# Products with V one unit later in the last third of the neighbourhood attention, and the weight groups' sums of squares moved into a score's bank

## The chip, the core and the metric

The kernel runs on one NeuronCore of a Trainium2 chip. The core has TensorE (PE, matrix products into PSUM), VectorE (DVE), ScalarE (ACT), GpSimd (POOL) and SyncE (SP, which here only issues DMAs). Each engine takes its instructions in the order in which the program gives them. The metric is the device time of one execution in microseconds (us); three executions of the kernel before gave 583.09, 578.28 and 580.79 us, median 580.79 us.

## The reference

One encoder layer over 1024 tokens of width 1024, cut to what matters here:

```python
def reference(x, norm_gain, w_in, q_norm_a, k_norm_a, na_rpb, w_out, final_norm_gain):
    h = _rmsnorm(x, norm_gain[l])
    proj = h @ w_in[l]
    q_a, k_a, v_a, g_a, q_b, k_b, v_b, g_b = jnp.split(proj, split_at, axis=-1)
    ...
    o_a = _gqa_blocked(q_a, k_a, v_a) * jax.nn.silu(g_a)
    o_b = _neighbourhood_attn(q_b, k_b, v_b, na_rpb[l])   # scores + bias, masked softmax, times V
    o_b = o_b * jax.nn.silu(g_b)
    mixed = jnp.concatenate([o_a, o_b], axis=-1)
    x = x + mixed @ w_out[l]
    return _rmsnorm(x, final_norm_gain)
```

Group A is full attention with 8 query heads over 2 key heads, group B attention over a window of the token grid with 8 heads of 64.

## The kernel before, in words

Every float32 operand of a product is split into two 16-bit parts, and a product is made of three 16-bit products (high·high, high·low, low·high). Weights come in 17 groups of 256 columns (0 to 12 from w_in, 13 to 16 from w_out), 1 MB each, loaded by POOL (L206) into two buffers. For each group ACT squares the raw weights in four quarters (`squares`, L349); PE adds the squares over the partitions with four one-column matmuls (`prep_b`, L364, "the sum"); DVE reads the result (L366) and POOL makes a scale of it (L367). Then ACT and DVE make the group's two parts (`split`, L390 and L395), and when these are done the next raw load may start.

After the projections and group A's attention comes group B's, in 64 *units*: one head of one block of 128 queries, the blocks in the order 0, 7, 1, 2, 3, 4, 5, 6 (`ORDER`), against 256 keys in the first 16 units and 384 in the rest. The program goes through *slots*; slot i does for unit i the softmax's first half (`b_qk`), for unit i-1 the rest (`b_lo`), and for unit i-5 the product with V (`b_pv`; 5 is `SKEW_B`). Step by step, for one unit:

- PE: scores, in every second slot for two units at once (`b_scores`, L801 and L804), each in one of four PSUM banks "sb";
- DVE: bias and maximum (L818), scale (L820); ACT: two exponentials (L821, L822); DVE: the low part (L827), into one of five buffers `t`;
- SP: a DMA transpose of both parts (L829) into one of five buffers `ptb`;
- PE: 6 or 9 matmuls with V (L842 to L844), four units in one of two PSUM banks "pvb"; after the fourth, DVE divides by the sums (L852 to L855) and POOL multiplies by the gate (L857). If the gate's part is not there yet, this evacuation is put off by a slot, and while it is, `late["held"]` keeps sums back.

When both halves of a block's mixed row are there, `os_start` squares, scales and splits the row (L880 to L898) and SP transposes it (L905). The output projection then multiplies it by the groups 13 to 16 (L480, tiles `po`), DVE adds the product to the residual (L953) and so frees the PSUM tile, of which there are two; ACT squares the row (L974), POOL takes the root (L982), DVE scales it (L985) and SP stores it (L986).

The order on PE is written by hand: in each slot the scores, then 2.4 *chunks* of six matmuls of pending projections ("fill"), then the product with V. A sum comes after the end of a tile or of a slot, if nothing is held, in the pvb bank that is not in use at the moment, in column 264+g (`spare[-1]`). ACT's and DVE's side work is handed out by a planner (`Flow`) that gives each slot a budget; what is due or urgent goes first. After the last unit a scheduler orders DVE, ACT, POOL and SP, and the fill that is left goes on: first the rows of block 4, then of 5 (`ORDER[5]`, `ORDER[6]`: blocks 4 and 5), at last of block 6, whose own row ends the kernel.

Of the kernel before, what the change touches and what calls it, by code (L numbers as in the profile page):

```python
# [16 lines left out]
P = 128  # L17
KC = 8
NU = 8
GC = 256  # L20
# [9 lines left out]
FILL_B = []  # L30
FILL_B_END = 2.4
SPLIT_AT = (8, 16, 24, 32, 40, 48, 56)
X2_BEHIND = {0: (0, 1), 1: (2,), 2: (3,), 3: (4,), 4: (5,), 5: (6,), 6: (7,)}
# [104 lines left out]
def kernel(ctx: ExitStack, tc: tile.TileContext, x: bass.AP, w: bass.AP, wo: bass.AP,  # L138
# [203 lines left out]
    def squares(g, delay):  # L342

        wss[g] = [tn(f"wss{g}_{k}", 1, "ws") for k in range(4)]

        def quarter(i):
            o = (carve(ar, 16384 + SLOTS["th"][0] + (turn.get("th", 0) + 1) % 2 * SLOTS["th"][1], [512], BF16)
                 if "b" in late else va_more)
            act.activation(o.rearrange("p (k c) -> p k c", c=GC), raw[g][:, QUARTERS[i]], AF.Square, accum_out=wss[g][i])  # L349
            if i == 3:  # L350
                job("act", 0, pend.append, g, delay=1, late=0, key=("sq", g))
        for i in range(4):
            job("act", 0.75 if g < 13 else 1.0, quarter, i, delay=delay, late=3 if g < 13 else 1.2, key=("sq", g))
# [4 lines left out]

    def prep_b(g):
        pt = spare[-1][:, 264 + g:265 + g]  # L360
        top = [a.bitcast(BF16)[:, 1:2] for a in (mh[:, :1], *wss[g])]
        n = len(wss[g])
        for i in range(n):
            pe.matmul(pt, top[0].to_broadcast([P, P]), top[1 + i], start=i == 0, stop=i == n - 1)  # L364
        t = wss[g][0]
        dve.tensor_scalar(t, pt, -2.0 ** -27, 1e-30, op0=OP.mult, op1=OP.add)  # L366
        pool.tensor_tensor(col(S_ + g), t, mh[:, :1], op=OP.pow)  # L367
        scaled.add(g)
# [82 lines left out]
    def sums_now(force=False):  # L451

        while pend and (force or late.get("head", 2) == 2 and (pend[0] < 3 or fl.slot >= late.get("again", 0)) and not late.get("held")):
            g = pend.pop(0)
# [339 lines left out]
    def b_scores(u, hs):  # L794
# [4 lines left out]
        for h in hs:  # L799
            sbs[u, h] = bank("sb")[:, :n * P]  # L800
            pe.matmul(sbs[u, h], q[h], khh[:, h, ks], start=True, stop=False)  # L801
        for h in hs:
            r = slice(h % 2 * D, h % 2 * D + D)
            pe.matmul(sbs[u, h], q[h][r], late["klo"][r, h // 2, ks], start=False, stop=True)  # L804

    def b_qk(i, u, h):
# [18 lines left out]
    def b_lo(i, u, h):  # L825
        hl, t = hls.pop(("b", u, h))
        dve.tensor_tensor(hl[:, 1], t, hl[:, 0], op=OP.subtract)  # L827
        pt = slot("ptb", [P, 2 * keys(u)[1], P], F16)
        sp.dma_start_transpose(pt, hl.rearrange("p a b -> p (a b)"))  # L829
        pts["b", u, h] = pt  # L830

    def b_pv(i, u, h):
# [12 lines left out]
        if h % 4 == 3:  # L845
            def evac():
                late["held"] = (u // 2, hh * GC) not in ready
                if late["held"]:
                    job("dve", 0.85, evac, late=0)
                    return  # L850
# [229 lines left out]

    def run_units(units, skew, qk, lo, pvf, n, hooks=None, by_hand=0):

        m, hand = len(units), ExitStack()
        for i in range(m + skew):
            if i == by_hand:
                hand.enter_context(tc.manual_schedule(engines={e.engine for e in (act, dve, pool, sp)}))
            first = (lambda: qk(i, *units[i])) if i < m else None
            second = (lambda: lo(i - 1, *units[i - 1])) if 1 <= i <= m else None
            last = (lambda: pvf(i - skew, *units[i - skew])) if i >= skew else None
            if qk is a_qk:  # L1090
# [65 lines left out]
    def hooks2(i):  # L1156
        hooks(i)
        for u, k in zip(ORDER, SPLIT_AT):
            if i - SKEW_B == k:
                at(1, "post", os_start, u)  # L1160
# [3 lines left out]
    fl.base = BASE_B  # L1164
    with run_units(ub, SKEW_B, b_qk, b_lo, b_pv, rates(FILL_B, FILL_B_END), hooks2):
        pass
# [92 lines left out]
```

## Time and profile before

| | |
|---|---|
| profiled execution, whole | 580.6 us |
| its span in the trace | 578.8 us |
| PE busy | 520.2 us, 90% |
| DVE busy | 458.5 us, 79% |
| ACT busy | 391.7 us, 68% |
| granted TensorE clock, mean | 0.972 of 2.4 GHz |
| group B's units, first scores to last | 370.4 to 520.8 us |

The engines' busy shares are averages over stages; group B's stage is read by itself below. In a timeline row the first number is the start in us from the span's start, the second the duration, the bracket the idle time of the engine before the row and what ended it.

### The profile page before, as it was taken

Reading aid. Unit: us, or ns where it says so; the run is one execution under the profiler, and the core shown is the slowest. Engines: PE = TensorE matmul, PEld = TensorE weight load, DVE = VectorE, ACT = ScalarE, POOL = GpSimd, SP = SyncE. Lnnn points to the kernel's source line nnn. Section 1 sums busy time; section 2 is a strip of 40 time slices with the busy share of each in tenths; the row PEclk is TensorE's granted clock in tenths of the full one; section 3 lists DMA queues with packets and bytes.
Section 4 is the critical chain, followed back from the end, with each engine's and each line's share of the span. In section 5 each row is a group of like instructions: output and inputs, shape, how many; then the busy total and the mean of one; then the engine's idle time right before and its main releaser. Section 6 shows DMA issues by size and latency. Waiting matters only on the chain. (4 is left out here: it accounts for less than half of the span.)

```text
span 578.8 us, 13970 instructions
## 1 busy us (share of the span) xinstructions
PE 520.2 (90%) x5583; PEld 404.1 (70%) x5583; DVE 458.5 (79%) x1018; ACT 391.7 (68%) x615; POOL 150.1 (26%) x181
## 2 busy tenths in 40 slices
PE   2678989969999999999999999997989988897894
PEld 0456867757887555568888888885867766786783
DVE  4688687989887987878789888577988998888742
ACT  5555456668777759686786867395889987775210
POOL 2395786650000000000000024333412220111300
PEclk9978999998999999999999999997989999999898
DMA  9989548779999999998999989234397999979732
GB/s 241 224 163 233 119 114 155 129 146 166 210 218 193 156 216 185 199 190 160 235 169 198 195 177 179 96 74 111 64 180 158 210 170 171 158 148 189 156 73 73
DMA packets 245539, 95.49 MB, mean 165 GB/s; under 512 B 236513, under 2 KB 237025, under 8 KB 243554
## 3 DMA queue, kind: packets, MB, share of 16 engines
q1 hardware_dynamic: 241874, 73.89, 71.5%
q0 software_dynamic: 3312, 19.92, 12.6%
q8 instruction: 43, 0.70, 0.5%
q10 hardware_dynamic: 288, 0.79, 0.5%
q14 instruction: 22, 0.18, 0.1%
HBM read 29.56 MB, written 4.19 MB: 58 GB/s over the span
## 5 line engine op out<-in xcount | busy, mean ns | idle before, releaser
L480 PE MATMUL pj<-whl,hT 128*128 128x256 f16 x2112 | 258.4, 280 | 22.1 <-DMA hT<-ar 7.5
L480 PEld LDWEIGHTS <-hT 128*128 128x128 f16 x2112 | 205.7, 100 | 61.6 <-issue 18.2
L720 ACT ACTIVATE ar<-s,nm,sm 128x1024 f32<-128x1024 f32 x64 | 76.9, 1201 | 55.6 <-DVE nm L718 55.3
L718 DVE CUSTOM_DVE_ANT_0 ar<-s,sm 128x1024 bf16<-128x1024 f32 x64 | 82.0, 1281 | 34.2 <-PE s L713 33.8
L480 PEld LDWEIGHTS <-ar 128*128 128x128 f16 x768 | 73.1, 99 | 16.1 <-issue 6.8
L726 DVE TENSOR_TENSOR ar<-ar 128x1024 f16<-128x1024 f32 x64 | 80.3, 1254 | 0.9 <-ACT ar L721 0.8
L480 PE MATMUL po<-whl,ar 128*128 128x256 f16 x576 | 70.0, 277 | 3.1 <-DVE x L953 2.3
L721 ACT ACTIVATE ar<-ar 128x1024 f16<-128x1024 f32 x64 | 67.6, 1057 | 1.9
L821 ACT ACTIVATE rq<-ar,mx,sm 128x384 f32<-128x384 f32 (+1 forms) x64 | 43.0, 672 | 25.0 <-DVE mx L820 25.0
L822 ACT ACTIVATE ar<-ar,mx,sm 128x384 f16<-128x384 f32 (+1 forms) x64 | 43.5, 680 | 2.1
L480 PE MATMUL kb<-hT,whl 128*128 128x512 f16 x192 | 44.5, 379 | 0.0
L711 PE MATMUL s<-kTa,rq 128*128 128x512 f16 x128 | 38.5, 383 | 2.6 <-ACT ar L720 2.4
L827 DVE TENSOR_TENSOR ar<-rq,ar 128x384 f16<-128x384 f32 (+1 forms) x64 | 35.7, 557 | 6.1 <-ACT ar L822 6.0
L744 PE MATMUL pv<-va,ar 128*128 128x64 f16 x384 | 40.3, 194 | 0.0
L743 PE MATMUL pv<-va,ar 128*128 128x65 f16 x384 | 40.2, 193 | 0.0
L745 PE MATMUL pv<-va,ar 128*128 128x65 f16 x384 | 40.0, 192 | 0.0
L743 PEld LDWEIGHTS <-ar 128*128 128x128 f16 x384 | 35.7, 97 | 5.5 <-issue 0.3
L744 PEld LDWEIGHTS <-ar 128*128 128x128 f16 x384 | 35.5, 97 | 5.5 <-issue 0.3
L395 DVE SCALAR_TENSOR_TENSOR whl<-raw,sm,whl 128x512 f16<-128x512 f32 x52 | 38.4, 771 | 0.2 <-ACT whl L390 0.2
L206 POOL DMA_DIRECT2D raw<-in_w_dram x11 | 6.7, 607 | 112.8 <-ACT ar L721 88.7
L745 PEld LDWEIGHTS <-ar 128*128 128x128 f16 x384 | 35.6, 99 | 0.0
L390 ACT ACTIVATE whl<-raw,sm 128x512 f16<-128x512 f32 x52 | 33.8, 708 | 0.0
(163 smaller groups left out, 916.1 us busy)
## 6 DMA issues: line engine op xcount, KB each, us to landing
raw<-in_w_dram POOLq DMA_DIRECT2D x11, 1024.0 KB, 7.7
raw<-in_wo_dram POOLq DMA_DIRECT2D x4, 1024.0 KB, 5.8
ar<-in_x_dram SPq DMA_DIRECT2D x7, 512.0 KB, 6.2
khh<-ar SPq DMA_DIRECT2D x16, 128.0 KB, 3.5
x2b<-in_x_dram POOLq DMA_DIRECT2D x4, 512.0 KB, 6.2
x<-in_x_dram POOLq DMA_DIRECT2D x4, 512.0 KB, 6.9
out_dram<-x2b SPq DMA_DIRECT2D x8, 256.0 KB, 3.5
ar<-ar SPq DMA_TRANSPOSE x112, 4.4
```

Of the source, the lines that this page charges most:

```text
L395: dve.scalar_tensor_tensor(wp[g][1][:, q], raw[g][:, q], col(S_ + g), wp[g][0][:, q], op0=OP.mult, op1=OP.subtract)
L480: pe.matmul(*o[0], **o[1])
L711: pe.matmul(s[:, c * 512:(c + 1) * 512], q, kTa[:, 4 * c:4 * c + 4, hh], start=True, stop=False)
L718: dve.tensor_tensor_reduce(out=hl[:, 1].bitcast(BF16), in0=s, in1=col(SHA).to_broadcast([P, 1024]), scale=col(NSA), scalar=3e38, op0=OP.ad ...
L720: act.activation(p32, s, AF.Exp, bias=nm, scale=col(SCA))
L721: at(0, "mid", lambda: act.activation(hl[:, 0], p32, AF.Copy))
L726: dve.tensor_tensor(hl[:, 1], p32, hl[:, 0], op=OP.subtract)
L743: pe.matmul(o, pt[:, kt], va[:, kt, hh, v_hi], start=kt == 0, stop=False)
L744: pe.matmul(o[:, :D], pt[:, kt], va[:, kt, hh, v_lo], start=False, stop=False)
L745: pe.matmul(o, pt[:, 8 + kt], va[:, kt, hh, v_hi], start=False, stop=kt == 7)
L821: act.activation(p32, t, AF.Exp, bias=mx, scale=col(SCB + hh))
L822: act.activation(hl[:, 0], t, AF.Exp, bias=mx, scale=col(SCB + hh))
```

## The change

Two things, and what they need.

1. From slot 40 on (`MORE`) the product with V of unit i-6 stands in slot i in place of i-5; slot 40 has none, and there is one slot more at the end. For the sixth transposed unit a buffer is added: every sixth unit from 40 on goes to the place of the second gate buffer "th", and from slot 38 on the squares' waste output keeps to the first.
2. In group B a sum is issued right behind a pair's scores, in the bank of the second of them (column 400+g), and no more at the end of tiles and slots. `late["held"]` goes; a group's sum may come two slots after its last square in place of one.

```diff
+MORE = 40
@@ squares
-            o = (carve(ar, 16384 + SLOTS["th"][0] + (turn.get("th", 0) + 1) % 2 * SLOTS["th"][1], [512], BF16)
+            o = (carve(ar, 16384 + SLOTS["th"][0] + (0 if "six" in late else (turn.get("th", 0) + 1) % 2) * SLOTS["th"][1], [512], BF16)
...
-                job("act", 0, pend.append, g, delay=1, late=0, key=("sq", g))
+                job("act", 0, pend.append, g, delay=2 if "b" in late else 1, late=0, key=("sq", g))
@@ prep_b
-    def prep_b(g):
-        pt = spare[-1][:, 264 + g:265 + g]
+    def prep_b(g, pt=None):
+        if pt is None:
+            pt = spare[-1][:, 264 + g:265 + g]
@@ sums_now
-        while pend and (force or late.get("head", 2) == 2 and (pend[0] < 3 or fl.slot >= late.get("again", 0)) and not late.get("held")):
+        while pend and (force or "b" not in late and late.get("head", 2) == 2 and (pend[0] < 3 or fl.slot >= late.get("again", 0))):
@@ b_scores
-            sbs[u, h] = bank("sb")[:, :n * P]
+            at_s = bank("sb")
+            sbs[u, h] = at_s[:, :n * P]
...
+        if pend:
+            g = pend.pop(0)
+            prep_b(g, at_s[:, 400 + g:401 + g])
+            try_split(g)
@@ b_lo
-        pt = slot("ptb", [P, 2 * keys(u)[1], P], F16)
+        k = i - MORE + 5
+        pt = (area(32896, [2 * keys(u)[1], P], F16) if k >= 0 and k % 6 == 5 else
+              slot("ptb", [P, 2 * keys(u)[1], P], F16))
@@ b_pv
-                late["held"] = (u // 2, hh * GC) not in ready
-                if late["held"]:
+                if (u // 2, hh * GC) not in ready:
@@ run_units
-        for i in range(m + skew):
+        for i in range(m + skew + (more < 1000)):
+            back = skew + (i >= more)
...
-            last = (lambda: pvf(i - skew, *units[i - skew])) if i >= skew else None
+            last = (lambda: pvf(i - back, *units[i - back])) if i >= back and i != more else None
@@ hooks2
+        if i == MORE - 2:
+            late["six"] = True
         for u, k in zip(ORDER, SPLIT_AT):
-            if i - SKEW_B == k:
+            if i - SKEW_B - (i >= MORE) == k:
                 at(1, "post", os_start, u)
```

The built order, at the three places of which the prediction speaks. First PE, where group 13's sum stands (`wss`: the squares' partial sums, `pvb` and `sb`: banks of the products with V and of the scores). Before, behind the product with V of slot 11, ahead of the scores of units 12 and 13:

```order
L844 MATMUL pvb_5110<-ar 128x65
L364 LDWEIGHTS mh
L364 MATMUL pvb_5109<-wss_0_5041,mh 128x1
L364 LDWEIGHTS mh
L364 MATMUL pvb_5109<-wss_1_5042,mh 128x1
...
L801 LDWEIGHTS qTb_109
L801 MATMUL sb_5107<-khh,qTb_109 128x256
```

Now, behind the scores of units 8 and 9:

```order
L807 LDWEIGHTS qTb_107
L807 MATMUL sb_5107<-klo,qTb_107 128x256
L366 LDWEIGHTS mh
L366 MATMUL sb_5107<-wss_0_5041,mh 128x1
L366 LDWEIGHTS mh
L366 MATMUL sb_5107<-wss_1_5042,mh 128x1
...
L482 LDWEIGHTS hT_99
L482 MATMUL pj_0_5293<-whl_4862,hT_99 128x256
```

It has moved up by almost four slots and out of the pvb bank. The others: group 12 from slot 7 to slot 0, group 14 from slot 23 to 18, group 15 from slot 27 to 24; group 16 from just ahead of slot 40's scores to just behind them. The four raw loads of w_out follow: on POOL the third stands now ahead of the first block's row scale (L887, L895 now), some four units earlier.

Second ACT, the squares of group 14 (`wss_0` to `wss_3`; `mx_h` names the unit by its head). Before:

```order
L349 ACTIVATE ar,wss_1_5419<-raw_5416 128x512
L821 ACTIVATE rq<-ar,mx_0_5642,sm 128x384
...
L349 ACTIVATE ar,wss_2_5420<-raw_5416 128x512
L821 ACTIVATE rq<-ar,mx_2_5720,sm 128x384
L822 ACTIVATE ar<-ar,mx_2_5720,sm 128x384
L349 ACTIVATE ar,wss_3_5421<-raw_5416 128x512
L821 ACTIVATE rq<-ar,mx_3_5746,sm 128x384
```

Now:

```order
L350 ACTIVATE ar,wss_2_5394<-raw_5390 128x512
L828 ACTIVATE rq<-ar,mx_6_5575,sm 128x256
L829 ACTIVATE ar<-ar,mx_6_5575,sm 128x256
L888 ACTIVATE mhl_5586,os_5585<-ar 128x512
L350 ACTIVATE ar,wss_3_5395<-raw_5390 128x512
L828 ACTIVATE rq<-ar,mx_7_5619,sm 128x256
```

The last square has moved from ahead of unit 19 to ahead of unit 15. Group 15's last square likewise stands now ahead of unit 21.

Third DVE at the end of the units (L852, now L860: evacuation of a pvb bank, `sumb_1` of the last four units; L953, now L961: residual, `po_15` of block 3). Before:

```order
L852 RECIPROCAL sumb_1_7657<-pvb_5110 128x4
L853 TENSOR_TENSOR sumb_1_7657<-sumb_1_7657,sm 128x4
L855 TENSOR_TENSOR ar<-pvb_5110,sumb_1_7657 128x256
L985 SCALAR_TENSOR_TENSOR x2b<-x2b,of_7002,gain_o 128x512 x2
L962 TENSOR_TENSOR rw_13_7586<-os_7130,sm 128x1
L953 SCALAR_TENSOR_TENSOR x_6421<-po_15_7483,rw_15_7484,x_6421 128x256 x2
```

Now:

```order
L961 SCALAR_TENSOR_TENSOR x_6421<-po_15_7470,rw_15_7471,x_6421 128x256 x2
...
L961 SCALAR_TENSOR_TENSOR x_6421<-po_13_7569,rw_13_7570,x_6421 128x256
L989 TENSOR_SCALAR of_6993<-of_6993 128x1
L860 RECIPROCAL sumb_1_7687<-pvb_5110 128x4
L993 SCALAR_TENSOR_TENSOR x2b<-x2b,of_6993,gain_o 128x512 x2
...
L961 SCALAR_TENSOR_TENSOR x_6421<-po_13_7569,rw_13_7570,x_6421 128x256
L989 TENSOR_SCALAR of_7495<-of_7495 128x1
L863 TENSOR_TENSOR ar<-pvb_5110,sumb_1_7687 128x256
```

The residual of block 3 stands now ahead of the last evacuation, not behind it, and the evacuation's last step stands behind one L993 pair more. On PE the product of unit 63 with V has 18 more fill matmuls ahead of it (12 and 6, of the rows of block 4), and 234 in place of 252 output matmuls behind it.

## Rows read from the trace of the kernel before

**Rows 1.** The waits of PE over the whole span: line, what was waited for, total us, times, longest.

```profile
PE pvb L842 <- DMA ar<-ar: 11.2, 7, 2.8
...
PE pvb L364 <- DVE ar L855: 3.0, 1, 3.0
```

**Rows 2.** Timeline of PE from slot 11's end to unit 16's scores.

```profile
397.14 0.25 PE L364 MATMUL pvb<-wss,mh 128*128 128x1 bf16 x4 [2.99 <-DVE ar L855]
397.25 0.59 PE L801 MATMUL sb<-khh,qTb 128*128 128x256 f16 x2
...
398.10 4.02 PE L480 MATMUL pj<-whl,hT 128*128 128x256 f16 x18
...
404.16 0.38 PE L801 MATMUL sb<-khh,qTb 128*128 128x256 f16 x2
...
408.34 0.49 PE L801 MATMUL sb<-khh,qTb 128*128 128x384 f16 x2
```

**Rows 3.** Busy time by stretch: PE, PEld, DVE, ACT, POOL (with instruction counts), granted clock, DMA share, GB/s. Columns: stretch, its length, then these.

```profile
397.00:404.10 7.10, 6.96 (x49) 4.86 (x49) 3.57 (x14) 3.42 (x7) 3.44 (x4) 0.57 0.30 55
...
542.60:549.60 7.00, 6.96 (x49) 5.59 (x49) 5.41 (x23) 2.77 (x6) 1.08 (x2) 0.76 0.56 161
```

**Rows 4.** Timeline of DVE ahead of the evacuation that PE waited for.

```profile
388.93 2.74 DVE L395 SCALAR_TENSOR_TENSOR whl<-raw,sm,whl 128x512 f16<-128x512 f32 x4 [0.19 <-ACT whl L390]
...
396.67 0.42 DVE L855 TENSOR_TENSOR ar<-pvb,sumb 128x256 f32<-128x256 f32 x1
```

**Rows 5.** Waits of DVE from 397 to 406 us, and its busy time there and in a later stretch, 468 to 525 us (columns as in rows 3).

```profile
DVE ar L685 <- ACT ar L680: 2.0, 1, 2.0
DVE ar L818 <- PE sb L804: 1.0, 2, 0.6
...
397.00:406.00 9.00, 8.86 (x66) 6.30 (x66) 4.67 (x18) 5.29 (x10) 4.97 (x6) 0.66 0.26 48
...
468.00:525.00 57.00, 52.56 (x604) 41.42 (x601) 50.12 (x165) 43.04 (x76) 9.85 (x14) 1.00 1.00 159
```

**Rows 6.** The third raw load of w_out on POOL; the time from issue to landing of the L829 transpose issued at 422.6 us, and of those from 374 to 420 us (min/median/max); PE around the product with V of that unit, 19.

```profile
421.79 0.62 POOL L206 DMA_DIRECT2D raw<-in_wo_dram  x1 [2.81 <-ACT ar L822]
...
DMA to landing us min/median/max: 8.2/8.2/8.2
...
DMA to landing us min/median/max: 2.4/2.4/4.1
...
425.42 0.49 PE L801 MATMUL sb<-khh,qTb 128*128 128x384 f16 x2
...
430.76 0.24 PE L842 MATMUL pvb<-rq,ar 128*128 128x65 f16 x1 [2.51 <-DMA ar<-ar]
...
434.08 0.49 PE L801 MATMUL sb<-khh,qTb 128*128 128x384 f16 x2
...
438.60 0.24 PE L364 MATMUL pvb<-wss,mh 128*128 128x1 bf16 x4
```

**Rows 7.** Four waits of PE after unit 40's scores, in the timeline: at the product of unit 49 with V, at a fill tile, and at the products of units 58 (slot 63) and 59 (slot 64).

```profile
505.76 0.20 PE L842 MATMUL pvb<-rq,ar 128*128 128x65 f16 x1 [1.63 <-DMA ar<-ar]
...
524.51 1.47 PE L480 MATMUL po<-whl,ar 128*128 128x256 f16 x12 [0.75 <-DVE x2b L953]
...
527.79 0.20 PE L842 MATMUL pvb<-rq,ar 128*128 128x65 f16 x1 [1.82 <-DMA ar<-ar]
...
531.57 0.20 PE L842 MATMUL pvb<-rq,ar 128*128 128x65 f16 x1 [1.36 <-DMA ar<-ar]
```

**Rows 8.** Waits of DVE from 460 to 530 us.

```profile
DVE ar L818 <- DMA ar<-ar: 3.2, 3, 2.1
DVE x2b L985 <- POOL of L982: 2.0, 3, 0.7
```

**Rows 9.** The end: PE behind the product of unit 63 with V, and DVE and SP there.

```profile
538.84 1.47 PE L480 MATMUL po<-whl,ar 128*128 128x256 f16 x12
...
539.86 1.87 DVE L985 SCALAR_TENSOR_TENSOR x2b<-x2b,of,gain_o 128x512 f32<-128x512 f32 x2
...
541.73 0.86 DVE L953 SCALAR_TENSOR_TENSOR x<-po,rw,x 128x256 f32<-128x256 f32 x2
...
542.64 7.07 PE L480 MATMUL po<-whl,ar 128*128 128x256 f16 x48 [2.33 <-DVE x L953]
...
548.00 2.88 SPq L905 DMA_TRANSPOSE ar<-mhl  x2
...
549.55 2.78 PE L480 MATMUL po<-rest,ar 128*128 128x256 f16 x24
...
552.17 8.02 PE L480 MATMUL po<-whl,ar 128*128 128x256 f16 x72
...
560.03 2.78 PE L480 MATMUL po<-rest,ar 128*128 128x256 f16 x24
```

**Rows 10.** ACT's exponentials of units 15 (409.13) and 21 (423.85), its last square of group 14, and the scores of units 18 and 19 on PE.

```profile
409.13 0.60 ACT L821 ACTIVATE rq<-ar,mx,sm 128x256 f32<-128x256 f32 x1 [0.37 <-DVE mx L820]
...
412.68 0.49 PE L801 MATMUL sb<-khh,qTb 128*128 128x384 f16 x2
...
419.61 0.61 ACT L349 ACTIVATE ar<-raw 128x512 bf16<-128x512 f32 x1
...
423.85 0.71 ACT L821 ACTIVATE rq<-ar,mx,sm 128x384 f32<-128x384 f32 x1 [0.29 <-DVE mx L820]
```

More of the change, by code (lines that the diff above doesn't have):

```diff
@@ L1079, with run_units @@
         mixA[up] = carve(ar, MIX + 4096 * up, [2, 512], F32)
-    def run_units(units, skew, qk, lo, pvf, n, hooks=None, by_hand=0):
+    def run_units(units, skew, qk, lo, pvf, n, hooks=None, by_hand=0, more=1000):
         m, hand = len(units), ExitStack()
-        for i in range(m + skew):
+        for i in range(m + skew + (more < 1000)):
+            back = skew + (i >= more)
             if i == by_hand:
@@ L1164 @@
     fl.base = BASE_B
-    with run_units(ub, SKEW_B, b_qk, b_lo, b_pv, rates(FILL_B, FILL_B_END), hooks2):
+    with run_units(ub, SKEW_B, b_qk, b_lo, b_pv, rates(FILL_B, FILL_B_END), hooks2, more=MORE):
         pass
```

## The prediction

> **What bounds the kernel now.** I read four views in this order: the waits of PE, its timeline at each of them, the busy time by stretch, and the timelines of DVE and ACT at the same places. In the whole span PE waits longest for transposed probabilities ahead of a product with V (11.2 us in seven waits), and once, 3.0 us, ahead of a sum, for DVE's evacuation of a pvb bank [rows 1]. In the last third of the units, from 468 to 525 us, PE is busy for 52.56 of 57 us and DVE for 50.12 [rows 5]. DVE's waits from 460 to 530 us name DMA and POOL, not PE [rows 8]. So there PE and DVE are close to equal, and a wait of PE that goes shortens the time only as far as DVE and the transposes can follow. Behind the product of unit 63 with V it is PE alone: 12 matmuls, a wait, then output matmuls to the end [rows 9].
>
> **Basis.** The profiled execution took 580.6 us (its span is 578.8, 1.8 lie around it); the median of the three runs is 580.79, 0.2 above. I subtract from 580.6.
>
> **Group 13's sum (first edit).** PE stood from 394.15 to 397.14 us for L855 [rows 2], which came late on DVE behind four L395 [rows 4]. The pair of slots that followed took from 397.25 to 404.16, 6.91 us, the next one with the same matmuls from 404.16 to 408.34, 4.18 us [rows 2]; the granted clock over it was 0.57, so for most of it the lower level of 1.2 GHz [rows 3]. The place costs 2.99 + (6.91 - 4.18) = 5.72 us. Now the sum stands four units earlier, in a score's bank. PE needs L855 next for unit 8's product with V, which writes the same pvb bank and closes the pair: at about 394.15 + 4.18 = 398.3, when L855 (ended 397.09 [rows 4]) is over. DVE was busy for 4.67 of the 9 us from 397 to 406 [rows 5], so 4.3 us there are free for it to move up, and 3.0 of its waits name PE or, by ACT, PE's late tile [rows 5]. The gain lies between 3.0 (only what DVE names) and 5.7 (all). I take **4.7**, nearer the upper end because the L395 of group 13 move into DVE's hole as well.
>
> **The third raw load (moved by the first edit).** It is issued at 421.79 us; the transpose issued at 422.6 landed 8.2 us later, where the median from 374 to 420 us was 2.4 [rows 6]. Unit 19's product with V waited 2.51 us for it, and its pair took from 425.42 to 434.08, 8.66 us, against 4.52 of the next (434.08 to 438.60) [rows 6]: 4.14 us. In the new order the load stands some four units earlier, where units still have 256 keys and less to transpose. Bounds: all 4.1 gained, or another unit meets the load and nothing is gained; a loss of the same size would need two units hit in place of one. I take **2.0**, the middle, as no row shows transposes of these units beside a load. The Trainium skill ("DMA: Bandwidth & Descriptors", Issuing engines are not separate DMA queues) says that DMAs from any engine end on the same 16 DMA engines and interleave. Rows 6 agree, and by that rule a load that is moved only moves its collision: this term would be 0 and the sum 571.6.
>
> **Sums ahead of the fill (cost of the first edit).** A sum now stops PE at the pair's scores if the group's last square is late, and behind it stand the pair's fill and its products with V; on DVE L366 stands ahead of both L818. The work is the same: four matmuls and one L366 for each group. Group 14's last square stands now ahead of unit 15's exponential, which ran at 409.13, and the scores it follows began at 412.68 [rows 10]: over 3 us to spare. Group 15's stands ahead of unit 21's, at 423.85 [rows 10], and its scores began at 425.42 [rows 6]: 1.6 us to spare, less what PE gains on ACT. I take **0.7 of cost**; bounds 0 and the second rival below.
>
> **Six units behind (second edit), slots 40 to 62.** A slot is 4.52 / 2 = 2.26 us [rows 6], and every wait for a transpose after 468 us is shorter than that (the longest are 1.63 and 1.82 [rows 7]). But DVE waits for the same transposes: L818 writes a buffer that unit i-5's transpose reads, and that ring stays at five; 3.2 us of DVE's time go there, 2.1 in one [rows 8]. At 524.51 PE waits for DVE's L953, which the skew does not touch [rows 7]: what PE has gained by then is waited for there. I take **0.5**; bounds 0 and 2.4 (1.63 + 0.75 [rows 7]).
>
> **The end.** Before, PE finished unit 63's product with V at 538.84, did 12 matmuls, waited 2.33 us for L953, which stood on DVE behind the last evacuation and L985 (539.86 to 541.73), and then needed 549.55 - 542.64 = 6.91 us for 48 matmuls [rows 9]; 24 take 552.17 - 549.55 = 2.62 us [rows 9], 48 so 5.24, and the difference, 1.67 us, is the clock (0.76 granted [rows 3]). Now L953 stands ahead of that evacuation: 2.33 + 1.67 = 4.0 us. Also 18 matmuls, 18 x 2.62 / 24 = 1.97 us, have moved from behind the product with V to ahead of it. They cover waits there: 1.82 and 1.36 us at the products of units 58 and 59 [rows 7], where unit 58's now comes a slot later and does not wait, and unit 59's, with 12 matmuls and one product with V more ahead of it, still waits some 1.9 us for the landing at 531.5. So unit 63's product ends at 538.84 - (1.82 + 1.36 - 1.9) + 1.97 = 539.5, 0.7 later, with 1.97 us less behind it. Together 4.0 + 1.97 - 0.7 = 5.3 us. What this may uncover: block 6's row. Its transposes were issued at 548.0 and done by 550.9, and PE began with it at 560.03 [rows 9], 9 us of cover. It shrinks by the 4.0, by the 1.97 and by what DVE's last evacuation comes later (L985, 1.87 us, stands now in it), to about 1 us. For L953s that come a little late I take off 0.8: **4.5**; bounds 1.0 (waits elsewhere on the two tiles) and 6.0 (4.0 and all of 1.97).
>
> **Sum.** 4.7 + 2.0 - 0.7 + 0.5 + 4.5 = 11.0 us: **569.6 us**. What else of the 11.2 us [rows 1] lies ahead of slot 40 stays; PE may even wait longer there if it comes earlier than its transposes, one more reason to count 4.7 of the 5.7.
>
> **Rivals.**
> *The transposes and DVE hold the time.* The first gain is the 3.0 that DVE names, the third load's collision reappears at another unit, the skew gives nothing in the slots, and at the end the last row's cover runs out or L953 is waited for again, which leaves 1.0, the lower bound there. For it: DVE at 50.12 of 57 us [rows 5], 8.2 us transposes beside loads [rows 6]. Against: the hole from 397 to 406, where all engines stood. 580.6 - 3.0 - 1.0 = 576.6.
> *Nothing is gained on balance*: as before, with a wait for a square or for block 6's row (2 to 3 us) besides. 579 to 581.
> *Slower: the sums wait for the squares.* If ACT, busy for 43.04 of 57 us after 468 [rows 5], does group 14's last square where it does now, at 419.61 + 0.8, and the scores end at 413.4 (412.68 + 0.7) [rows 10], PE stands for 7.0 us and then loses 2.73 to the clock as in rows 2, 9.7 in all; group 15, with less to spare, the same. All of PE's fill and, through L366, DVE stop too. 580.6 - 4.7 - 4.5 + 2 x 9.7 = 590.8. It decides once the two waits exceed the gains, 9.2 us and more. Against: the squares moved up with the sums. The Trainium skill ("PSUM — Partial Sum Buffer", PSUM bank collisions raise a hardware error) has it that PSUM is guarded by bank and quadrant, not by address. The wait of the sum for L855, which reads other columns [rows 2], agrees; by that rule a late sum keeps DVE from the second score of its pair in any case, whatever the order on DVE.
> *More*: both uncertain terms at their upper ends (5.7 and 4.1, the end 6.0): 564 and below.
>
> **Chances and range.** About 1% is what a measurement of this kernel can tell from no change (5.8 us: under 574.8 and over 586.6). Forecast 0.56 (565 to 574.5), transposes and DVE 0.22 (574.5 to 579, of it 0.03 under 574.8), nothing 0.11, slower 0.07, more 0.04. Faster 0.56 + 0.04 + 0.03 = 0.63, slower 0.07, within 0.30. The range leaves out the slower case, most of the "more", and little else: 563 to 581.
>
> **What the profile of the changed kernel would show.** Step one: no wait of PE for L855 at a sum, the pair of units 12 and 13 in about 4.2 us, granted clock near 1.00 there. Load: no 2.5 us wait at unit 19, or the same wait at an earlier unit. Squares: no wait of a sum for ACT. Skew: PE's waits for transposes after unit 40 down from the 4.8 us of rows 7 to about 2. End: no wait for L953 behind the last product with V, its product at half clock gone, block 6's row without a wait. Wrong it would be if PE waits as long, with other names, or if DVE in 468 to 525 us has not moved up by some 6 us.

## The result and the profile after

| | before | changed |
|---|---|---|
| median of the timed runs | 580.02 us (578.28 to 583.09) | 571.88 us (571.09 to 572.66) |
| ratio, 95% interval | | 0.9889 (0.9845 to 0.9933) |
| span of the profiled execution | 578.8 us | 570.8 us |
| matmuls on PE, granted clock over the span | 5583 | 5583, 0.979 |

The kernel became 1.1% faster, some 8 us; the forecast was 11.0 us, 569.6. Medians and ratios here and below are of fast runs, so that a run of more than 1.5% above the fastest of its kernel is left out. In the experiments below, whose rounds ran the kernel before beside them, the changed kernel had 571.19 us and a ratio of 0.9895 (0.9850 to 0.9939). The changed file is longer, so line numbers are shifted: L842 (product with V) is L851 now, L364 (sum) L366, L480 (fill) L482, L685 L687, L801 L804, L818 L825, L829 L838, L855 L863, L905 L913, L953 L961, L985 L993, L206 L207, L395 L397, L772 (GpSimd's additions of a mask) L774, L827 L834.

The waits of PE over the span of the changed kernel (total, times, longest), where [rows 1] had 11.2 us in seven waits for transposes and 3.0 for L855:

```profile
PE pvb L851 <- DMA ar<-ar: 5.5, 4, 2.3
...
PE pj L482 <- DVE ar L687: 3.2, 2, 2.9
PE po L482 <- DVE x2b L961: 1.8, 2, 1.5
```

The wait of the sum for the evacuation is gone, and the waits for transposes are halved. But a wait of 2.9 us has come that was not there: a fill tile waits for VectorE's L687, which frees the accumulator bank of the fill tile before it. The timeline of PE in the changed kernel from unit 12's scores on, the place of [rows 2]:

```profile
392.96 0.38 PE L804 MATMUL sb<-khh,qTb 128*128 128x256 f16 x2
...
398.01 0.20 PE L851 MATMUL pvb<-rq,ar 128*128 128x65 f16 x1 [0.90 <-DMA ar<-ar]
...
398.21 0.38 PE L804 MATMUL sb<-khh,qTb 128*128 128x256 f16 x2
...
402.50 0.48 PE L804 MATMUL sb<-khh,qTb 128*128 128x384 f16 x2
...
408.07 0.25 PE L366 MATMUL sb<-wss,mh 128*128 128x1 bf16 x4
...
414.10 1.44 PE L482 MATMUL pj<-whl,hT 128*128 128x256 f16 x6 [2.94 <-DVE ar L687]
415.67 0.83 PE L804 MATMUL sb<-khh,qTb 128*128 128x384 f16 x2
```

The pair of units 12 and 13 takes 398.21 - 392.96 = 5.25 us now, 0.90 of it a wait for transposes, against 6.91. Then, two pairs on, PE stands for 2.94 us, and the six matmuls that follow take 1.44 us where six elsewhere take 0.82 (a row of the end, below). The busy time by stretch (columns as in [rows 3]):

```profile
397.00:405.00 8.00, 7.11 (x79) 5.63 (x78) 7.69 (x22) 5.52 (x12) 4.25 (x4) 1.00 0.34 68
405.00:411.00 6.00, 5.61 (x61) 4.55 (x59) 5.89 (x16) 4.97 (x11) 5.30 (x7) 1.00 0.41 107
...
414.10:419.10 5.00, 5.00 (x40) 3.40 (x40) 4.83 (x16) 3.06 (x8) 2.94 (x3) 0.69 0.73 158
```

From 397 to 411 VectorE, the third column behind the length, is busy for 7.69 + 5.89 = 13.58 of 14 us: the hole of [rows 5] is full, and VectorE is what PE runs into. After the wait the granted clock is 0.69, between the two levels of 1.2 and 2.4 GHz. So what was removed at 397 us is paid again at 414.

To see the gain along the way, this table gives the start of the scores of some units, in us from the scores of unit 0 of group B (which began at 370.44 us before and 369.90 in the changed kernel; that part is untouched and varies by some us from run to run), and then one length. The kernels below the second row are those of the experiments; "changed, again" is a second profile of the changed kernel.

| | unit 12 | 20 | 28 | 36 | 40 | 62 | 62 to the span's end |
|---|---|---|---|---|---|---|---|
| before | 26.8 | 46.6 | 68.3 | 85.7 | 97.8 | 150.2 | 58.1 |
| changed | 23.1 | 45.8 | 63.8 | 87.1 | 97.0 | 146.7 | 54.2 |
| changed, again | 23.1 | 47.6 | 66.3 | 85.2 | 98.7 | 148.0 | 54.4 |
| sums only | 23.1 | 45.8 | 63.9 | 87.1 | 97.0 | 149.1 | 57.6 |
| skew only | 26.8 | 45.7 | 66.2 | 84.9 | 98.8 | 150.5 | 53.1 |
| skew at 63 only | 26.8 | 45.8 | 66.3 | 85.1 | 99.4 | 149.7 | 56.8 |
| no mask additions | 23.1 | 42.4 | 59.8 | 82.7 | 93.0 | 143.4 | 54.1 |
| mask later | 23.1 | 42.8 | 60.3 | 83.9 | 94.0 | 145.2 | 54.1 |
| mask later, again | 23.1 | 42.5 | 60.0 | 82.3 | 97.3 | 146.2 | 54.7 |

One profile against another of the same kernel differs by up to 3.3 us at unit 40, so a single entry is read no finer than that; the last column repeats within 0.6. At unit 12 the changed kernel is 3.7 us ahead, at unit 16 5.3, at unit 20 0.8 ahead in one profile and about 1 behind in the other, and at unit 40 again 0.8 ahead and 0.9 behind. Up to slot 38 the two kernels without the sums ("skew only", "skew at 63 only") run in the order of the kernel before, and by them the lead at unit 16 is 4.0 to 4.1. The mean start of unit 40 is 98.7 us in the three profiles with the order of before and 97.5 in four with the sums moved (the three in the table and the kernel with the skew from 56, 97.2). So of the 6.0 us that the prediction counted ahead of slot 40, some 1 us is left there, less than one profile tells from another. The end gives 3.8 to 3.9.

At unit 28 a second part goes. The load of the fourth group of wo on GpSimd's queue, the times to landing of the two transposes issued from 441.5 to 444.0 (minimum, median, maximum), and the product of unit 28 with V:

```profile
443.25 0.62 POOL L207 DMA_DIRECT2D raw<-in_wo_dram  x1 [8.51 <-issue]
...
DMA to landing us min/median/max: 2.7/4.6/6.5
...
450.56 0.20 PE L851 MATMUL pvb<-ar 128*128 128x65 f16 x1 [2.34 <-DMA ar<-ar]
```

This is what [rows 6] showed at unit 19 with the third load. Unit 19 does not wait any more; unit 28 does, for 2.34 us, and over the 4.5 us behind it the granted clock is 0.62:

```profile
450.50:455.00 4.50, 4.44 (x30) 2.92 (x31) 3.82 (x12) 4.43 (x9) 0.88 (x1) 0.62 1.10 176
```

With it the lead over the one profile of before goes from 4.4 us at unit 28 to 1.4 us of lag at unit 36. What the wait is worth farther on is asked in the experiments.

The end, the place of [rows 7] and [rows 9]: PE, and VectorE's evacuation of the fill tile.

```profile
521.26 1.47 PE L482 MATMUL po<-whl,ar 128*128 128x256 f16 x12 [1.54 <-DVE x2b L961]
...
528.18 0.20 PE L851 MATMUL pvb<-rq,ar 128*128 128x65 f16 x1 [1.62 <-DMA ar<-ar]
...
535.57 0.82 PE L482 MATMUL po<-whl,ar 128*128 128x256 f16 x6 [0.23 <-DVE x L961]
...
536.50 4.75 PE L482 MATMUL po<-whl,ar 128*128 128x256 f16 x42
541.08 2.78 PE L482 MATMUL po<-rest,ar 128*128 128x256 f16 x24
...
552.40 2.56 PE L482 MATMUL po<-rest,ar 128*128 128x256 f16 x22 [0.46 <-DMA ar<-mhl]
...
534.66 0.86 DVE L961 SCALAR_TENSOR_TENSOR x<-po,rw,x 128x256 f32<-128x256 f32 x2
...
536.80 1.39 DVE L993 SCALAR_TENSOR_TENSOR x2b<-x2b,of,gain_o 128x512 f32<-128x512 f32 x2
```

L961 runs at 534.66, ahead of the last evacuation and of L993, and PE waits for it by 0.23 us instead of 2.33. The matmuls behind the last product with V start at once, and 42 take 4.75 us, so the half clock there is gone too. Block 6's row, late by 0.46, has lost its cover.

### The profile page after: what moved, and what is told of

Same layout as the page of the kernel before. It is cut to its first block, busy times and chain, and to the rows that moved or that the text cites. A ratio compares the mean times of both kernels' runs of the same rounds, so it can differ in the third digit from the quotient of the medians.

```text
span 570.8 us, 13962 instructions
## 1 busy us (share of the span) xinstructions
PE 517.2 (91%) x5583; PEld 402.1 (70%) x5583; DVE 459.4 (80%) x1018; ACT 391.7 (69%) x615; POOL 150.6 (26%) x181
## 5 line engine op out<-in xcount | busy, mean ns | idle before, releaser
L482 PE MATMUL pj<-whl,hT 128*128 128x256 f16 x2112 | 254.9, 278 | 26.1 <-DMA hT<-ar 9.2
L482 PEld LDWEIGHTS <-hT 128*128 128x128 f16 x2112 | 203.7, 99 | 63.6 <-issue 20.3
L482 PEld LDWEIGHTS <-ar 128*128 128x128 f16 x768 | 73.0, 99 | 16.1 <-issue 7.0
L482 PE MATMUL po<-whl,ar 128*128 128x256 f16 x576 | 68.7, 273 | 2.0 <-DVE x2b L961 1.8
L829 ACT ACTIVATE ar<-ar,mx,sm 128x384 f16<-128x384 f32 (+1 forms) x64 | 43.5, 680 | 2.1
L482 PE MATMUL kb<-hT,whl 128*128 128x512 f16 x192 | 44.5, 379 | 0.0
L834 DVE TENSOR_TENSOR ar<-rq,ar 128x384 f16<-128x384 f32 (+1 forms) x64 | 35.5, 555 | 8.2 <-ACT ar L829 8.0
L397 DVE SCALAR_TENSOR_TENSOR whl<-raw,sm,whl 128x512 f16<-128x512 f32 x52 | 39.5, 790 | 0.0
L207 POOL DMA_DIRECT2D raw<-in_w_dram x11 | 6.7, 607 | 113.0 <-ACT ar L723 88.8
```

Of the source, the lines that this page charges most:

```text
L397: dve.scalar_tensor_tensor(wp[g][1][:, q], raw[g][:, q], col(S_ + g), wp[g][0][:, q], op0=OP.mult, op1=OP.subtract)
L482: pe.matmul(*o[0], **o[1])
L829: act.activation(hl[:, 0], t, AF.Exp, bias=mx, scale=col(SCB + hh))
```

## The experiments

Twelve runs were made, in three groups of four; the kernels of a group shared the rounds of the kernel before (medians of 577.73, 577.47 and 576.67 us), except one that ran for its profile alone. Kernels of different groups are compared by their ratios. Diffs are against the changed kernel unless it is said otherwise.

### Which part carries the gain

The sums alone:

```diff
-MORE = 40
+MORE = 1000
```

> The sums in the scores' bank alone; products with V stay five units behind to the end. Theory A (the sums' gain is given back ahead of slot 40, since DVE sets the pace there; the skew and the end carry the result): 578 to 580.5 us, at most 2 us below before; PE reaches unit 40's scores 0 to 2 us earlier than before, the wait of 2.3 us for L953 behind the last product with V is back. Rival B (the sums carry the result): 573 to 576 us, 4 us or more below before.

Measured 576.34 us, ratio 0.9965 (0.9940 to 0.9991), some 2.0 us below before: the edge of theory A (at most 2), whose time in us was set too high, and not rival B. From unit 0 to unit 40 it stands like the changed kernel (97.0); from unit 62 on it needs 57.6 us, and the wait for L961 is there again (the second row is the busy time behind it, columns as in [rows 3]):

```profile
540.50 5.40 PE L482 MATMUL po<-whl,ar 128*128 128x256 f16 x48 [2.33 <-DVE x L961]
...
540.50:545.70 5.20, 5.20 (x48) 4.67 (x48) 4.62 (x22) 2.76 (x6) 1.08 (x2) 1.00 0.23 70
```

The wait is as long as before and at the same place, but the granted clock behind it is 1.00 here, where [rows 3] have 0.76. So the half clock before was no sure consequence of this wait.

The skew alone, with the sums as before:

```diff
-                    job("act", 0, pend.append, g, delay=2 if "b" in late else 1, late=0, key=("sq", g))
+                    job("act", 0, pend.append, g, delay=1, late=0, key=("sq", g))
...
-            while pend and (force or "b" not in late and late.get("head", 2) == 2 and (pend[0] < 3 or fl.slot >= late.get("again", 0))):
+            while pend and (force or late.get("head", 2) == 2 and (pend[0] < 3 or fl.slot >= late.get("again", 0)) and not late.get("held")):
...
-        if pend:
-            g = pend.pop(0)
-            prep_b(g, at_s[:, 400 + g:401 + g])
-            try_split(g)
...
-                if (u // 2, hh * GC) not in ready:
+                late["held"] = (u // 2, hh * GC) not in ready
+                if late["held"]:
```

> Six units behind from slot 40 on alone; sums where they were before. Theory A: 572 to 574.5 us, 6 to 8 us below before: the 3.0 us wait for the evacuation at slot 12 and the 2.5 us wait at unit 19 are back, and by slot 40 nothing is lost by it. Rival B: 576 to 579 us.

Measured 572.13 us, 0.9894 (0.9851 to 0.9936), the same as the whole change can be told to be, and as theory A had it; the waits of 2.99 us for the evacuation and of 2.18 at unit 19 are back. So the skew carries most of the gain. The moved sums are worth some 2 us by themselves; beside the skew (0.9894 without them, 0.9889 and 0.9895 with them) the times show nothing of it.

The skew at the last unit alone (the kernel above with one number changed):

```diff
-MORE = 40
+MORE = 63
```

> As the skew alone, but begun at slot 63, so that in the slots 40 to 62 the products stand five units behind, and only the end has the extra slot. If the end is worth what the traces show from unit 62's scores on (4.0 us) and the slots the rest: 575.5 to 577.5 us, 2.5 to 4.5 below before. If the skew in the slots is needed for the end's gain (the transposes waited for in slots 63 and 64): within 1.5 us of before.

Measured 577.55 us, 1.0000 (0.9978 to 1.0023): nothing, so the second of the two expectations holds. PE's wait at the end, and VectorE there, in this kernel (L958 is L961):

```profile
541.69 1.26 PE L482 MATMUL po<-whl,ar 128*128 128x256 f16 x6 [2.77 <-DVE x L958]
...
539.37 1.42 DVE L990 SCALAR_TENSOR_TENSOR x2b<-x2b,of,gain_o 128x512 f32<-128x512 f32 x2 [1.09 <-POOL of L987]
...
540.76 0.87 DVE L958 SCALAR_TENSOR_TENSOR x<-po,rw,x 128x256 f32<-128x256 f32 x2
```

The last product with V does stand a slot later, but the wait has only moved ahead of it: L958 still stands on VectorE behind L990, which itself waits for GpSimd. One number more asks how much skew the end needs:

```diff
-MORE = 40
+MORE = 56
```

> The changed kernel with MORE = 56 instead of 40: the sums as in the change, six units between scores and products only from unit 56 on. Theory Q (the end's gain needs no more than that the products of the last units stand six behind before the last slots, so that the waits at units 58 and 59 go and L961 stands ahead of them): units 62 to the span's end take 54 to 55 us as in the changed kernel, slots 40 to 56 as in the kernel with the sums alone, and the time is 572.5 to 575 us. Rival (the lead gathered in slots 40 to 56 is what carries the end): units 62 to the end take 56.5 us and more, 575 to 577 us.

Measured 572.84 us, 0.9925 (0.9896 to 0.9954); 53.7 us from unit 62 to the end, as in the changed kernel (54.2) or better, though PE waits 1.68 us for L961 there (at 538.82). The time is theory Q's, but not that step of it. From unit 40 to unit 62 it needs 53.8 us against 49.8 (52.0 with the sums alone), with a wait of 2.64 us at a product with V at 472.60. So the end needs the skew from some units before it (56 is enough, 63 is not), and not the lead of slots 40 to 56.

### Why the sums' gain does not last

VectorE in the changed kernel at group 13's L397, and GpSimd's additions of the inner mask to the scores' bias, L774, beside them:

```profile
397.62 0.74 DVE L397 SCALAR_TENSOR_TENSOR rest<-raw,sm,rest 128x512 f16<-128x512 f32 x1
...
399.20 2.90 DVE L397 SCALAR_TENSOR_TENSOR rest<-raw,sm,rest 128x512 f16<-128x512 f32 x2
...
405.45 1.48 DVE L397 SCALAR_TENSOR_TENSOR rest<-raw,sm,rest 128x512 f16<-128x512 f32 x1
...
406.93 0.40 DVE L825 CUSTOM_DVE_ANT_0 ar<-sb,rq 128x256 f32<-128x256 f32 x1
...
398.91 2.64 POOL L774 TENSOR_TENSOR ar<-ar,rest 128x384 f32<-128x384 f32 x2
...
405.21 1.18 POOL L774 TENSOR_TENSOR ar<-ar,rest 128x384 f32<-128x384 f32 x1
406.34 1.45 POOL L774 TENSOR_TENSOR rq<-rq,rest 128x384 f32<-128x384 f32 x1
```

An L397 takes 0.74 us by itself and 1.48 to 1.49 beside an L774. Before, group 13's L395 ran later, and only one of these four, the first of the two at 406.36, stood beside such an addition (1.49 us):

```profile
406.36 2.15 DVE L395 SCALAR_TENSOR_TENSOR rest<-raw,sm,rest 128x512 f16<-128x512 f32 x2
...
413.50 0.74 DVE L395 SCALAR_TENSOR_TENSOR rest<-raw,sm,rest 128x512 f16<-128x512 f32 x1
...
420.50 0.74 DVE L395 SCALAR_TENSOR_TENSOR rest<-raw,sm,rest 128x512 f16<-128x512 f32 x1
```

The theory: this keeps VectorE late, and by that PE waits for L687. The first look takes the additions away:

```diff
-        pool.tensor_tensor(bias[hh][:, h4i], bias[hh][:, h4i], late["inner"], op=OP.add)
```

> The changed kernel without the eight additions on POOL that narrow the bias mask for the inner blocks (L774); this part of the mask is left out. Theory A1 (DVE could not use the hole because its L397 run beside POOL's L774 and take 1.49 us there in place of 0.74): the four L397 of group 13 take 0.74 each, PE's wait of 2.9 us for L687 at slot 19 shrinks to under 1.5 us and PE reaches unit 20's scores 1.5 to 3.5 us earlier than in the changed kernel. Rival A2 (DVE is late by its amount of work alone): L397 at 0.74 or not, the wait at slot 19 stays over 2 us.

One execution took 565.35 us, too few and with too little work to compare; what counts is the trace. Unit 20 comes after 42.4 us instead of 45.8, PE has no wait for L687 from 400 to 420 us, and group 13's four are at their own duration (two of the rows, the second of two instructions):

```profile
392.48 0.74 DVE L397 SCALAR_TENSOR_TENSOR rest<-raw,sm,rest 128x512 f16<-128x512 f32 x1
394.07 1.41 DVE L397 SCALAR_TENSOR_TENSOR rest<-raw,sm,rest 128x512 f16<-128x512 f32 x2
```

Without the additions VectorE has no less to do itself, so what it gained came from GpSimd. Two kernels do the additions in another way. On VectorE:

```diff
-        pool.tensor_tensor(bias[hh][:, h4i], bias[hh][:, h4i], late["inner"], op=OP.add)
+        dve.tensor_tensor(bias[hh][:, h4i], bias[hh][:, h4i], late["inner"], op=OP.add)
```

> The eight additions of the inner mask (L774) are done by VectorE instead of GpSimd. Theory P (GpSimd's tensor operations beside L397 slow VectorE, and by that make TensorE wait 2.94 us for L687 at slot 19): all of group 13's L397 take 0.74 us instead of 1.49, which saves VectorE some 2.3 us, but eight additions of some 0.5 us each come to it in the same slots, so the lead of TensorE at unit 20 is at most 2 us greater than in the changed kernel and may be the same: 569 to 573 us. Rival (VectorE's queue has no part in it, something else holds L687): the durations of L397 change and the wait at slot 19 stays 2.5 to 3 us, the time the changed kernel's within 0.5 us.

And on GpSimd, four slots later:

```diff
-        if NH < i <= 2 * NH:
-            at(1, "post", narrow, i - NH - 1)
+        if NH + 4 < i <= 2 * NH + 4:
+            at(1, "post", narrow, i - NH - 5)
```

> The eight additions of the inner mask stay on GpSimd, four slots later (slots 14 to 21 instead of 10 to 17), so that most of them stand behind group 13's L397. Theory P: three or four of group 13's last four L397 take 0.74 us, VectorE is 1.5 to 2.3 us earlier at slot 19, the wait for L687 there falls from 2.9 to under 1.5 us, and unit 20 comes 2 to 3 us earlier; what is left at the end is 1 to 3 us: 568.5 to 571 us, unless the additions now come too late for the units 16 to 23 that read the mask (then VectorE waits for GpSimd at L825 by 1 us and more, and the time is 571 to 575). Rival (L397's doubling is not the cause): the wait for L687 stays over 2.5 us.

The changed kernel ran in the same rounds:

> The changed kernel itself, on the chip and in the rounds of the three kernels beside it: 570 to 573 us. From the first scores of group B's unit 0 to the span's end about 201 us.

It had 571.19 us, 0.9895 (0.9850 to 0.9939), and 202.4 us from unit 0 to the span's end. On VectorE: 573.07 us, 0.9927 (0.9898 to 0.9956). Group 13's L397 took 0.74 to 0.75 us, the additions 0.55 us (two of them 1.0 to 1.1), the wait for L687 fell to 1.66, so that the rival falls, and unit 20 came after 43.8 us, 2 ahead of the changed kernel; nothing of that is left in the time. Four slots later: 570.16 us, 0.9867 (0.9822 to 0.9912). VectorE and PE there:

```profile
396.92 1.40 DVE L397 SCALAR_TENSOR_TENSOR rest<-raw,sm,rest 128x512 f16<-128x512 f32 x2
...
401.67 1.48 DVE L397 SCALAR_TENSOR_TENSOR rest<-raw,sm,rest 128x512 f16<-128x512 f32 x1
...
410.15 0.82 PE L482 MATMUL pj<-whl,hT 128*128 128x256 f16 x6 [0.26 <-DVE ar L687]
```

Three of the four are at their own duration, the wait for L687 is 0.26 instead of 2.94, the matmuls behind it run at full clock, and unit 20 comes 3 us earlier. That settles the wait at slot 19. In the time 1.0 us of the 3 is seen, less than these intervals separate; the kernel ran once more in the third group:

> The kernel with the mask four slots later once more, in the rounds of the kernels beside it: 569 to 571 us.

569.04 us, 0.9860 (0.9817 to 0.9903): both times the fastest of the complete kernels tried, though these intervals overlap with the changed kernel's.

The Trainium skill ("SBUF — State Buffer", Who interferes with whom) says that a VectorE instruction with two inputs in SBUF contends with a GpSimd instruction that reads SBUF. The same page (Summary: rules for kernel authors) says that the second of them to issue is blocked until the first finishes. The rows agree with both. L397 and L774 have two such inputs each, while L825, which reads its scores from PSUM, stays at 0.40 us beside an L774. The L397 in the rows above that start behind an L774 end 0.54 to 0.55 us after it, at 402.10 (401.55) and 406.93 (406.39), so most of the 0.74 us of an L397 by itself comes only then. And the L774 that starts at 406.34, while an L397 runs, takes 1.45 us, where the one at 409.57, which starts ahead of a VectorE subtraction (L834), takes 0.99.

### The wait at unit 28

The same load, some slots later:

```diff
-                at(1, "pre", load_w, g + 2)
+                at(5 if g == 14 else 1, "pre", load_w, g + 2)
```

> The changed kernel with the load of the fourth group of wo (1 MB, at 443.25 in the profile of the changed kernel) some four slots later, at about 453. Theory R: the transposes of unit 28 land some 2.4 us after their issue and its products wait under 0.5 us; the products of a unit between 31 and 34 wait for their transposes instead, by 1 to 2.5 us, and the sum of waits for transposes and the time stay within 1.5 us of the changed kernel. Rival (the landing of unit 28's transposes has nothing to do with the load): the wait at unit 28 stays at 2 us or more.

The load was issued at 449.88 us. The landing of the transposes issued from 441.5 to 444.1 and of those from 447.9 to 452.1, and PE:

```profile
DMA to landing us min/median/max: 2.7/2.8/2.8
...
DMA to landing us min/median/max: 6.5/7.1/7.8
...
457.84 0.20 PE L851 MATMUL pvb<-ar 128*128 128x65 f16 x1 [2.77 <-DMA ar<-ar]
```

Unit 28 does not wait, unit 31 waits for 2.77 us: the wait belongs to the load and goes where it goes. Unit 36 comes after 83.0 us, 4.1 earlier than in the changed kernel, but unit 40 after 98.3, no earlier (97.0 and 98.7 there). The time did not do what was expected: 574.55 us, 0.9963 (0.9923 to 1.0004), against 0.9895, where its profiled span, 572.3, is like the changed kernel's. What costs the timed runs more than that isn't known.

Does one more slot of skew cover this wait? The skew from unit 33 on, in the changed kernel and in the one with the mask later:

```diff
-MORE = 40
+MORE = 33
```

> The changed kernel with MORE = 33 and nothing else. Theory R: the wait of the products of unit 28 (2.34 us) falls below 0.7, unit 40 comes 1 to 3 us earlier after group B's unit 0 than the 96.95 to 98.70 us of the two profiles of the changed kernel, and the time is 0.5 to 2.5 us below it. Rival: within 0.5 us of 571.5.

> The kernel with the mask four slots later, and the six units of skew from unit 33 on instead of unit 40. Theory R (the wait of 2.26 us of the products of unit 28, and those of the units behind it, are the transposes' landing behind the load of the fourth group of wo; one slot more covers them): the products of unit 28 stand a slot later and wait under 0.7 us, unit 40 comes 1.5 to 3 us earlier after group B's unit 0 than in the kernel with the mask later alone (93.95 us there), and the time is 1 to 2.5 us below that kernel's in the same rounds. Rival (what is not waited for there is waited for by slot 36 at VectorE's output, since its queue is as late): unit 40 within 1 us of 93.95 and the time within 0.7 us.

Measured 575.67 us, 0.9964 (0.9929 to 0.9999), and 573.99 us, 0.9959 (0.9933 to 0.9985): both slower than with 40. The second, in the same rounds as the mask later with the skew from 40, is 4.9 us above it; the first is 4.5 us above the changed kernel of the group before (0.9964 against 0.9895). In both, unit 28's wait is gone. In the first, unit 36 comes after 83.0 us instead of 87.1 or 85.2, but unit 40 after 96.8, against 97.0 and 98.7, so the 1 to 3 us expected there are not shown (0.1 against the one, 1.9 against the other); in the second, unit 40 comes after 93.95 us, as in the kernel with the mask later, which is what the rival had. What was gained is given back, in output tiles (the first kernel):

```profile
464.23 0.38 PE L482 MATMUL po<-rest,ar 128*128 128x256 f16 x2 [2.71 <-DVE x2b L961]
465.37 1.01 PE L482 MATMUL po<-rest,ar 128*128 128x256 f16 x4 [0.76 <-DMA ar<-mhl]
...
484.14 0.39 PE L482 MATMUL po<-rest,ar 128*128 128x256 f16 x2 [0.71 <-DMA ar<-mhl]
486.91 0.60 PE L482 MATMUL po<-rest,ar 128*128 128x256 f16 x4 [2.38 <-DMA ar<-mhl]
```

The four sum to 6.56 us, 3.47 of it ahead of unit 40 and 3.09 behind it. The first is for VectorE's evacuation of the tile before, which PE, 2 to 4 us earlier at unit 36, has caught up with. The others are the row's own input. A block's output row can start only when its last product with V is evacuated; with the skew from unit 33 on the block of units 24 to 31 is a slot later, its transposes (L913) were issued at 478.54 instead of 474.01, and PE waits for them at 484.14 and 486.91. Behind the first two waits the granted clock is 0.61 (466.7 to 472.9), and the pair of units 40 and 41 takes 6.18 us instead of 3.69. Theory R was right on the stall and wrong on the sum: a term that I had not seen, the row's own deadline.

## Why the prediction was right or wrong

The time (571.9, forecast 569.6, range 563 to 581) and its sign came out; the shares of the parts did not. That the sum is off by only 2.3 us is in part luck: the terms ahead of slot 40 were some 5 us too high, and the slots from 40 to 62 gave more than forecast.

- **Group 13's sum, 4.7.** The mechanism at the sum was right: no wait of the sum for the evacuation, and the clock full; the pair took 5.25 us, though, not some 4.2, since unit 8's product with V waits there (0.90 for its transposes, in the second profile 0.64 for the evacuation L863). The 2.73 us that I counted for the clock are those of one profile: in the two kernels without the sums the same pair, behind the same wait of 2.99, took 5.60 and 5.75 us, not 6.91. The step that failed is "4.3 us there are free for it to move up", and with it "nearer the upper end because the L395 of group 13 move into DVE's hole as well". They did move, beside GpSimd's additions, where three of four took twice their time; VectorE came too late for the fill tile at slot 19, and 2.94 us and a stretch at a clock of 0.69 were paid; with three of the four at their own duration the wait is 0.26. Of a lead of 4.0 to 5.3 us at unit 16 nothing stood for certain at unit 20. I had charged the move at the durations of [rows 4], taken where GpSimd ran no addition; the 1.49 us of the L395 at 406.36 stood in the same trace.
- **The third load, 2.0.** Unit 19's wait went, as the step says; in the first profile its new neighbours did not wait (the slowest transpose landed in 5.6 us), in the second unit 14 waited 1.70 us (9.0). And PE, earlier now, met the fourth load at unit 28 for 2.34 us. The waits show the bound of 0, not the middle. The rule of the Trainium skill ("DMA: Bandwidth & Descriptors", Issuing engines are not separate DMA queues) would have made this term 0 and the sum 571.6, and the experiment with the later load shows just that of the fourth load: the landing goes from 6.5 to 2.8 us at one place and from 6.5 to 7.8 at the other. That 571.6 is close to the measured 571.9 shows nothing, since other terms were off by more.
- **Sums ahead of the fill, -0.7.** No wait of a sum for a square or for ACT in the changed kernel; the margins of [rows 10] sufficed, and the slower rival fell. The price is not seen by itself.
- **Skew in slots 40 to 62, 0.5.** The waits for transposes went from the 4.8 us of [rows 7], which leave out one of 0.86 at 485.87, to 1.62 (at 528.18), near the forecast of 2; units 40 to 62 take 49.8 and 49.3 us instead of 52.4, 2.6 to 3.1 less, above my bound of 2.4. With the skew alone it is 51.7, and with hardly any skew 50.2, so how much of it is the skew's isn't settled. That a kernel which comes late to unit 40 catches up behind it would explain this, but no run shows it by itself.
- **The end, 4.5.** Measured 3.9 and 3.8 of unit 62 to the end, 5.0 with the skew alone. The steps held: L961 ahead of the evacuation, no half clock, six matmuls in 0.82 us, block 6's row uncovered by 0.46. But the 1.67 us for the half clock are not shown to go with the wait: with the sums alone the wait of 2.33 us stood there, and the clock behind it was full. The last product with V came 1.7 us later from unit 62 on instead of 0.7, and PE waited for L961 at 521.26 for 1.54, twice the 0.75 of before. What I had not argued is that this needs the skew in the units ahead: the kernel with it at unit 63 alone has the wait still.

In sum the parts ahead of unit 62 gave 2.2 to 3.5 us of the 6.5 forecast, the end 3.9 of 4.5. Run by themselves, the sums are worth 2.0 us and the skew 6.1, by their ratios to 577.73: the reverse of my weights, 6.0 to 5.0. The rival "the transposes and DVE hold the time" described the first part better than my forecast did; what it had wrong was the end. Of the two signs of being wrong that the prediction names, the first is met in part: at slot 19 PE waits 2.94 us under another name, as long as the 2.99 that went, though its waits for transposes are halved. The second is met: VectorE's first step for unit 60 (L818, now L825) starts at 519.15 instead of 522.39, 3.2 us earlier, 1.6 in the second profile, not some 6. Two small slips of the prediction change nothing: 1% above 580.6 is 586.4, not 586.6, and the pair behind unit 19's took 4.63 us from scores to scores, since 438.60 is the start of a sum.

## What to carry over

A wait that is removed early in a long chain is worth only what the next-slowest engine lets through: count that engine's work at the durations it has where it will run, beside its new neighbours, not where it ran before. A load that is moved takes its neighbours' stall along, and a deeper skew makes everything that hangs on the last product, here the output rows, a slot later. The gain at the very end, behind which nothing waits, came nearly in full, once the units ahead of it were a slot deeper too.

## What the runs showed of the hardware

- VectorE's instructions with two inputs in SBUF took longer beside GpSimd's additions: L397 1.48 to 1.49 us instead of 0.74, and the 128x256 subtraction L834 once 1.22 (at 409.64) instead of 0.42. The kernel before has it too: an L395 of 1.49 at 406.36, a subtraction of 1.18 at 410.99.
- A wait of PE often had a second price behind it. In the kernel before the granted clock was 0.53 from 430.7 to 434.0, behind the wait of 2.51 us at unit 19; in the changed kernel it was 0.69 behind the wait of 2.94 us and 0.62 behind that of 2.34; with the later load 0.57 from 457.8 to 461.0, behind the wait of 2.77. But it stayed at 1.00 behind the waits of 1.54 and 1.62 us at the end, and with the sums alone behind one of 2.33 (540.5 to 545.7), after it had been 0.61 behind one of 1.98 (527.7 to 531.0), so the length of the wait alone does not tell. In the changed kernel the pair of units 18 and 19 held 2.94 us of idle time and 5.34 us of work, which took 4.78 with the mask later. I had priced this at the place it was removed and at the end, but not at the places where a wait could come back.
